# A fused matmul and rotary embedding: a new order in the head, and two more block pairs

## The chip, the core and the metric

The kernel runs on one core of a Trainium2 chip. The metric is the device time of one execution in microseconds (us), lower is better. Times before: 151.65 us median of three runs, 151.28 to 151.76. The engines are named as in the profile: PE (TensorE, matrix products; PEld are its weight loads), DVE (VectorE), ACT (ScalarE), POOL (GpSimd) and SP (SyncE, which here only issues DMAs).

## The reference

`x` is 16 x 512 x 768, `weight` 768 x 768, `cos` and `sin` 512 x 64, all float32; there are 12 heads of 64 columns.

```
y = np.matmul(x, weight).reshape(16, 512, 12, 64)
y1, y2 = y[..., :32], y[..., 32:]
out1 = y1 * cos1 - y2 * sin1      # cos1, sin1: the first 32 columns
out2 = y2 * cos2 + y1 * sin2      # cos2, sin2: the last 32
out  = np.concatenate([out1, out2], axis=-1).reshape(16, 512, 768)
```

Cosine and sine depend on the position in the sequence only, not on the batch or the head.

## The kernel before

**Tiles and groups.** The 8192 rows are cut into 64 tiles of 128 rows; a tile holds every fourth position of one batch, so that one set of cosine and sine rows serves it (`where`, L188). Four tiles, one from each of four batches, make a group; there are 16 groups. A group's result is 3072 columns wide and fills six banks of PSUM (`py`, L173). A tile needs six products of 128 rows of depth (`CHUNKS`, L133) for its 768 columns.

**The way of one tile.** SP loads it as float32 into one of ten buffers (`load`, L201). ACT casts it to float16 (`cast`, L236). PE transposes it in six 128 x 128 blocks (`turn`, L244) or, in the steady part, in twelve 64 x 64 blocks on two halves of the array's rows (`turn_rows`, L256). ACT copies it from PSUM (L185). PE multiplies it with the weights. DVE reads the banks and multiplies by cosine and by sine (`rope`, L412); POOL adds the two (L429), which gives the output in one of five buffers `ov`; ACT, at the end SP, stores it (`store`, L443).

**Block pairs.** Where `BLOCKS` (L137) names the second half of a group, its two tiles go another way. They are loaded in four quarters, permuted by the DMA, by SP in float32 (`xb`, then a cast on ACT, `cast_pair`, L274) or by POOL with the cast in the DMA (`xh`). DVE then transposes 32 x 32 blocks in one instruction (`turn_pair`, L282), into `xp`. PE does no transposes for them. Before, groups 5 to 14 have such a half, odd groups by SP, even ones by POOL.

**The order of products.** From tile 4 to tile 57 PE works in a row form (`walk`, `one`, `both`, L342 to L388): each product of depth 128 is split into two of depth 64, which run side by side on the two halves of the array's rows. The first half of the rows goes through three banks in the order 0, 1, 2, the second in the order 2, 0, 1 and 1024 columns later (`LAG`, L339). When both have finished a bank, `rope` is written for it: a unit of 512 columns and one of 1024 in each half of a group. Group 0 (`mm0`, L519) and the end run on the full array (`mm_piece`, L330).

**What sets the order around it.** Everything is written out by hand, in one list per engine; each engine works in order, and `Flow` (L17) places semaphores where data or buffers need them. In the loop over tiles (L639) `turns` writes transposes ahead by `T_AHEAD` = 3, `casts` by `C_AHEAD` = 5, `bturns` the block transposes of DVE by `B_AHEAD` = 4, `pool_loads` by `P_AHEAD` = 20, and `stores` (L607) holds the tile at which each store is issued. Loads of SP are written as buffers become free (`pump`, L491), in the order of `fetch` (L475).

**The head.** SP loads tiles 0 and 1, then weights and tiles in the order of L463, then cosine and sine, then the rest. Twelve products of zeros (`warm`) run first. Weight pieces are cast by DVE as they land, and group 0's products follow piece by piece. DVE makes the table of cosine and signed sine (`csn`, L557 to L561) ahead of the first `rope`.

**Buffers of the products.** `rope` writes its two products to `tq`, or to the space of the raw weights; from group 1 on there are three such buffers for halves of groups (`HOMES`, L171), so the products of one half wait for the additions of the half three before.

Of the kernel before, what the change touches and what calls it, by code (L numbers as in the profile page):

```python
# [12 lines left out]
MULT = mybir.AluOpType.mult  # L13
# [92 lines left out]
def kernel(  # L106
# [28 lines left out]


    BLOCKS = {}  # L137
    for g in range(5, 15):
        BLOCKS[g, 1] = "pool" if g % 2 == 0 and g >= 4 else "sp"

    def sbuf(name, shape, dt):
# [29 lines left out]
    HOMES0, HOMES, HOMESL = (0, 1024, 3072, 4096), (6144, 0, 3072), (0, 1024, 2048, 3072, 4096, 5120)  # L171
# [129 lines left out]
    def units(g):  # L301
        if g < LAST:
            cut = [2560] if g == LAST - 1 else []
            at = [0, 512, 1536, 2048] + cut + [3072]
            return [(c, z, py[:, c:z], [f"ps{b}" for b in range(c // 512, z // 512)],
                     "dve" if (g, c) == (LAST - 1, 2560) else "pool")
                    for c, z in zip(at, at[1:])]
        u = [(c, c + 512, py[:, c : c + 512], [f"ps{c // 512}"], "pool")
             for c in range(0, 2048, 512)]
        if g == LAST:  # L310
            for k, (home, bank) in enumerate([
                (py[:, 2048:2304], "ps4"), (py[:, 2560:2816], "ps5"),
                (pt_b[0][:, 0:256], "pt0"), (pt_b[1][:, 0:256], "pt1"),
            ]):
# [79 lines left out]
    def rope(g, u):  # L394
# [4 lines left out]
        if adder == "dve" and g == LAST:  # L399
            k = len(late)  # L400
            tq, keys = xs_b[k][:, 0 : 2 * w].rearrange("p (j n) -> p j n", j=2), [f"xs{k}"]
        elif 0 < g < LAST:
            lo = c0 % 1536
            if lo == 0:
                tq_of[0] = HOMES[ring("tq", len(HOMES))]
            tq, keys = products(tq_of[0], 1536, lo, lo + w)
            if tq_of[0] >= 6144:
                keys = keys + W_HOME
        else:
            homes = HOMESL if g else HOMES0  # L410
            tq, keys = products(homes[ring(f"tq{g}", len(homes))], w, 0, w)
        do("dve", lambda eng: eng.tensor_tensor(  # L412
            out=tq.rearrange("p j (h d) -> p j h d", d=D),
            in0=ps.rearrange("p (h d) -> p h d", d=D)
            .unsqueeze(1).broadcast_to((P, 2, nh, D)),
            in1=csn[:, :, r, :].unsqueeze(2).broadcast_to((P, 2, nh, D)),
            op=MULT), reads=banks + ["csn"], writes=keys)
        if g not in ov_of:
            ov_of[g] = ring("ov", NOV)
        o = ov_of[g]  # L420
# [39 lines left out]
        out=ident, in_=ident, compare_op=mybir.AluOpType.not_equal, fill=1.0,  # L460
        base=0, pattern=[[-1, P]], channel_multiplier=1), writes=["ident"])

    order = [0, 1, "w0", 2, "w1", "w2", 3, "w3", "w4", "w5"]  # L463
    for k in order:
        if isinstance(k, int):
            load(k)
        else:
            load_w(CHUNKS[int(k[1])])
    do("sp", lambda eng: eng.dma_start(
        out=csn[:, 0], in_=cos.rearrange("(p r) d -> p r d", r=SB)), writes=["cos"], dma="cos")  # L470
    do("sp", lambda eng: eng.dma_start(
        out=sin_sb, in_=sin.rearrange("(p r) d -> p r d", r=SB)), writes=["tq23"], dma="sin")
# [14 lines left out]
    fetched = [0]  # L487
    xs_used, xb_used = [0], [0]
    xs_sent, xb_sent = [4], [0]

    def pump():  # L491

# [12 lines left out]
                load_quarter(*j)  # L505
            fetched[0] += 1

    WARM = 12
    warmed = [0]

    def warm(k):
# [15 lines left out]
    def castx(i, e):  # L527
        cast(i, e)
        xs_used[0] += 1
# [3 lines left out]
    castx(0, "act")  # L533
    turn(0, "dve")
    castx(1, "act")
    warm(3)
    turn(1, "dve")
    castx(2, "act")
    cast_w(CHUNKS[0], "dve")
    for i in (0, 1):  # L540
        mm0(i, CHUNKS[0])
    turn(2, "act")
    castx(3, "act")
    for c in CHUNKS[1:3]:
        cast_w(c, "dve")
        for i in (0, 1):
            mm0(i, c)
    for c in CHUNKS[:2]:
        mm0(2, c)
    turn(3, "act")  # L550
    mm0(2, CHUNKS[2])
    for c in CHUNKS[3:5]:
        cast_w(c, "dve")
        for i in (0, 1, 2):
# [3 lines left out]
        out=csn[:, 1, :, 0:HD], in_=sin_sb[:, :, HD:D]), reads=["tq23"], writes=["csn1"])  # L558
    do("dve", lambda eng: eng.tensor_scalar_mul(
        out=csn[:, 1, :, HD:D], in0=sin_sb[:, :, 0:HD], scalar1=-1.0),  # L560
        reads=["tq23", "csn1", "cos"], writes=["csn"])  # L561
    assert not quarters
    pump()

    rows_on = [False]
    state = {"cast": 4, "turn": 4, "bturn": 0, "pool": 0}
    pairs = sorted(BLOCKS)
    pool_pairs = [p for p in pairs if BLOCKS[p] == "pool"]

# [50 lines left out]
    ROWS = QB * LAST - 2  # L620

    for i in (0, 1):
        mm0(i, CHUNKS[5])
    rope(0, U0[0])
    rope(0, U0[1])
    mm0(2, CHUNKS[5])
    rope(0, U0[2])
    casts(6)
    for c in CHUNKS[:3]:
        mm0(3, c)  # L630
    turns(5)
    for c in CHUNKS[3:5]:
        mm0(3, c)
    turns(6)
    mm0(3, CHUNKS[5])
    rope(0, U0[3])
    casts(8)

    for i in range(QB, NTILE):  # L639
        g, s = divmod(i, QB)  # L640
        us = units(g)
        done_to = (s + 1) * H
        rows_on[0] = QB <= i <= QB * LAST
        if i < ROWS:
            if s % 2 == 0:
                for r in range(2):
                    lines[r].extend(walk(i // 2, r))
            for n in range(1, 4):
                both((i - QB) * 4608 + n * 1536)
                if n == (1 if i > QB else 2):  # L650
                    turns(i + T_AHEAD, 1)
        if i == ROWS:
            both(NTILE * 4608)
        for n, p in enumerate(pieces(g, s)) if i >= ROWS else ():
            a, z, _, bank = p
            if n == 1 and i < QB * LAST:
# [62 lines left out]
```

## Time and profile before

| | |
|---|---|
| profiled execution | 151.73 us |
| its span, first to last instruction | 149.9 us |
| granted TensorE clock | 0.986 |
| PE, PEld busy | 140.8, 111.5 us (94%, 74%) |
| DVE, ACT, POOL busy | 126.4, 78.2, 122.8 us (84%, 52%, 82%) |
| DMA | 51.28 MB, mean 342 GB/s |

Shares are averages over a head, a steady part and a tail. What a stage is bounded by is read from what ends the waits there: the chain of waits gives that in order of time, and the timelines give each engine's work with the idle time before it and who ended it. Lines of a timeline are start, duration, engine, line, operation, tiles, shape and count; several instructions of one kind that follow each other are merged.

### The profile page before, as it was taken

The numbers are of one execution on the slowest core, as the hardware profiler recorded it, in microseconds if no ns is written. First come the engines' busy times: TensorE is split into PE (matmuls) and PEld (weight loads), VectorE is DVE, ScalarE is ACT, GpSimd is POOL, SyncE is SP. The second block draws the span as 40 slices with busy tenths as digits, with TensorE's granted clock in tenths as the row PEclk, the third lists the DMA queues.
The fourth block names the chain that finished last, engine by engine and source line by source line (L and its number), as shares of the span: only waits on it lengthen the run. The fifth ranks groups of instructions, "written<-read, shape, count | busy, mean of one in ns | idle before, by whom it ended". The sixth has DMA issues, their size and how long they took to land.

```text
span 149.9 us, 4381 instructions
## 1 busy us (share of the span) xinstructions
PE 140.8 (94%) x1926; PEld 111.5 (74%) x1926; DVE 126.4 (84%) x92; ACT 78.2 (52%) x92; POOL 122.8 (82%) x68
## 2 busy tenths in 40 slices
PE   6879999999999999999999999999999999999930
PEld 2435578888888888888888888888888888756620
DVE  0245998887888899999989998999989998999980
ACT  3453898778777924466262916093445626264000
POOL 1000396999989989999999999999996979999990
PEclk9999999999999999999999999999999999999995
DMA  4999999999999999999999999999999989996683
GB/s 129 343 398 402 405 398 397 319 380 341 333 358 389 357 354 325 380 397 279 330 361 407 262 346 352 363 321 333 365 364 387 388 338 390 393 387 240 247 314 105
DMA packets 27875, 51.28 MB, mean 342 GB/s; under 512 B 7504, under 2 KB 13392, under 8 KB 27856
## 3 DMA queue, kind: packets, MB, share of 16 engines
q1 hardware_dynamic: 14592, 27.92, 53.8%
q10 hardware_dynamic: 7824, 21.11, 36.0%
q0 software_dynamic: 5440, 1.97, 10.6%
q8 instruction: 15, 0.25, 0.7%
q14 instruction: 4, 0.03, 0.1%
HBM read 27.79 MB, written 25.17 MB: 353 GB/s over the span
## 4 chain that ended last, share of the span: by engine, by line
PE 79%; DVE 6%; DMA 4%; POOL 3%; issue 2%; SPq 1%; POOLq 0%
PE py L360 70%; DMA w_raw<-in_weight_dram 4%; PE py L335 4%; PE pt L266 4%; POOL ov L429 3%; DVE w_raw L412 2%; DVE tq L412 2%; SPq L205 1%; PE pt L251 1%; DVE ov L429 1%; SPq L227 1%; POOLq L675 0%; DVE w_sb L185 0%; SPq L714 0%; SPq L116 0%
## 5 line engine op out<-in xcount | busy, mean ns | idle before, releaser
L429 POOL TENSOR_TENSOR ov<-tq 128x1536 f32<-128x1536 f32 (+3 forms) x31 | 77.4, 2516 | 19.4 <-DVE tq L412 19.3
L360 PE MATMUL py<-w_sb,xt 64*128 64x512 f16 (+1 forms) x864 | 81.3, 323 | 0.0
L412 DVE TENSOR_TENSOR tq<-py,csn 128x1024 f32<-128x1024 f32 (+2 forms) x46 | 74.6, 1655 | 5.3 <-PE py L360 4.9
L360 PEld LDWEIGHTS py<-w_sb,xt 64*128 64x128 f16 x864 | 60.3, 94 | 10.7 <-DVE tq L412 0.4
L185 ACT COPY xt<-pt 128x768 f16<-128x768 f16 x42 | 33.5, 799 | 50.1 <-PE pt L266 48.8
L185 ACT CAST xc<-xs 128x768 f16<-128x768 f32 x44 | 38.9, 904 | 9.4 <-DMA xs<-in_x_dram 7.1
L360 PE MATMUL py<-w_sb,xp 64*128 64x512 f16 (+1 forms) x432 | 42.6, 323 | 0.0
L412 DVE TENSOR_TENSOR w_raw<-py,csn 128x1024 f32<-128x1024 f32 (+1 forms) x21 | 35.2, 1676 | 3.7 <-PE py L360 3.5
L429 POOL TENSOR_TENSOR ov<-w_raw 128x1536 f32<-128x1536 f32 (+1 forms) x11 | 33.8, 3073 | 3.2 <-DVE w_raw L412 3.2
L360 PEld LDWEIGHTS py<-w_sb,xp 64*128 64x128 f16 x432 | 30.7, 94 | 5.1
L335 PE MATMUL py<-w_sb,xt 128*128 128x256 f16 (+1 forms) x90 | 15.7, 323 | 1.4 <-DVE w_sb L185 1.1
L266 PEld LDWEIGHTS pt<-ident,xc 64*128 64x128 f16 x456 | 14.8, 95 | 1.7 <-ACT xc L185 0.6
L266 PE MATMUL pt<-ident,xc 64*128 64x64 f16 x456 | 14.8, 190 | 0.0
L335 PEld LDWEIGHTS py<-w_sb,xt 128*128 128x128 f16 x90 | 8.1, 98 | 7.1 <-DVE w_sb L185 2.7
L220 POOL DMA_DIRECT2D xh<-in_x_dram x20 | 11.7, 592 | 0.0
L185 ACT CAST xd<-xb 128x1536 f16<-128x1536 f32 x5 | 8.2, 1634 | 0.0
L185 DVE CAST w_sb<-w_raw 128x768 f16<-128x768 f32 x6 | 3.4, 558 | 3.6 <-DMA w_raw<-in_weight_dram 3.6
L294 DVE STREAM_TRANSPOSE xp<-xh 128x768 f32<-128x768 f32 x5 | 6.2, 1243 | 0.0
L514 PE MATMUL py<-tq 128*128 128x512 f16 x12 | 4.9, 570 | 1.4 <-DVE tq L457 1.4
L185 DVE COPY xt<-pt 128x768 f16<-128x768 f16 x2 | 1.1, 557 | 5.2 <-PE pt L251 5.2
L294 DVE STREAM_TRANSPOSE xp<-xd 128x768 f32<-128x768 f32 x5 | 4.8, 968 | 0.0
L335 PE MATMUL py<-w_sb,xp 128*128 128x512 f16 (+1 forms) x24 | 4.2, 327 | 0.0
(20 smaller groups left out, 18.1 us busy)
## 6 DMA issues: line engine op xcount, KB each, us to landing
xs<-in_x_dram SPq DMA_DIRECT2D x44, 384.0 KB, 16.5
out_dram<-ov ACTq DMA_DIRECT2D x41, 384.0 KB, 7.4
out_dram<-ov ACTq DMA_DIRECT2D x6, 768.0 KB, 6.3
xb<-in_x_dram SPq DMA_DIRECT2D x20, 192.0 KB, 16.1
out_dram<-ov SPq DMA_DIRECT2D x4, 768.0 KB, 5.1
w_raw<-in_weight_dram SPq DMA_DIRECT2D x6, 384.0 KB, 7.2
xh<-in_x_dram POOLq DMA_DIRECT2D x20, 96.0 KB, 12.3
out_dram<-ov SPq DMA_DIRECT2D x1, 384.0 KB, 2.9
```

Of the source, the lines that this page charges most:

```text
L185: eng.copy(out=o, in_=i_) if e == "act" else eng.tensor_copy(out=o, in_=i_)
L205: do(e, lambda eng: eng.dma_start(out=xs_b[k], in_=x[b].rearrange("(p r) h -> r p h", r=SB)[r]), writes=[f"xs{k}"], dma=f"xs{k}")
L220: do(e, lambda eng: eng.dma_start(out=dst[ts(q, R)], in_=src[r, q]), writes=[f"{name}q{q}"], dma=name)
L227: do(e, lambda eng: eng.dma_start(out=w_raw[:, t, h], in_=wv[t, h]), writes=[f"wr{t}{h}"], dma=f"w{t}{h}")
L251: do("pe", lambda eng: eng.transpose(pt[:, t, h, :], src[:, t, h, :], ident), reads=[f"xc{c}", "ident"], writes=[f"pt{k}"], tick=(t, h) == ...
L266: do("pe", lambda eng: eng.transpose(pts[r][:, t, h, :], src[rows, t, h, :], ident[rows, rows]), reads=[f"xc{c}", "ident"], writes=[f"pt{r ...
L294: do("dve", lambda eng: eng.transpose(out=dst, in_=src), reads=rd, writes=[f"xp{z}"])
L335: do("pe", lambda eng: eng.matmul(ps, get(t, h), w_sb[:, t, h, a - s * H : z - s * H], start=start, stop=stop), reads=[key, f"w{t}{h}"], w ...
L360: do("pe", lambda eng: eng.matmul(py[:, a:z], get(t, h)[rows], w_sb[rows, t, h, a - s * H : z - s * H], start=start, stop=not opens and en ...
L412: do("dve", lambda eng: eng.tensor_tensor(out=tq.rearrange("p j (h d) -> p j h d", d=D), in0=ps.rearrange("p (h d) -> p h d", d=D) .unsque ...
L429: do(adder, lambda eng: eng.tensor_tensor(out=ov_b[o][:, ds(c0, w)].rearrange("p (h t d) -> p h t d", t=2, d=HD), in0=tq[:, 0].rearrange(" ...
L514: do("pe", lambda eng: eng.matmul(py[:, ts(b, 512)], cold[:, 0:P], cold, start=True, stop=warmed[0] < WARM - 6), reads=["tq0"], writes=[f" ...
```

## The change

- **Loads.** Tile 4 is loaded behind the last weight piece, ahead of sine and cosine, and sine goes ahead of cosine. The table's two parts have keys of their own, so that the first `rope` waits for both parts and for cosine.
- **Head.** One warm product less; the first weight cast goes ahead of the copy of tile 1; tile 2 gets its third weight piece with tiles 0 and 1. Tile 5 is cast by POOL. Tile 4 is transposed in the middle of tile 3's products.
- **Group 0** has six `rope` units of 512 columns instead of 512, 1024, 512 and 1024, with bank 5 ahead of bank 4.
- **Group 1** begins on the full array: tiles 4 and 5 (`FIRST` is 6) are written by `mm_piece`, and the transposes of tiles 5, 6 and 7, in the form of `turn_rows`, stand between their products. The row form begins with tile 6.
- **Block pairs** begin with group 3: the second halves of groups 3 (by SP) and 4 (by POOL) are added. Up to tile 18 (`EVEN`) the block transposes are written one tile later, and transposes and casts are placed by even and odd tiles.
- **Stores.** Up to group 9, store number k is issued at tile 12 + k; before, at tile 5 + 47 k / 40, rounded down.

```diff
-    for g in range(5, 15):
+    for g in range(3, 15):
         BLOCKS[g, 1] = "pool" if g % 2 == 0 and g >= 4 else "sp"
...
             at = [0, 512, 1536, 2048] + cut + [3072]
+            if g == 0:
+                at = [*range(0, 3073, 512)]
...
-            homes = HOMESL if g else HOMES0
-            tq, keys = products(homes[ring(f"tq{g}", len(homes))], w, 0, w)
+            tq, keys = products(HOMESL[ring(f"tq{g}", len(HOMESL))], w, 0, w)
...
-            op=MULT), reads=banks + ["csn"], writes=keys)
+            op=MULT), reads=banks + ["cos", "csn1", "csn2"], writes=keys)
...
-    order = [0, 1, "w0", 2, "w1", "w2", 3, "w3", "w4", "w5"]
+    order = [0, 1, "w0", 2, "w1", "w2", 3, "w3", "w4", "w5", 4]
...
     do("sp", lambda eng: eng.dma_start(
+        out=sin_sb, in_=sin.rearrange("(p r) d -> p r d", r=SB)), writes=["tq23"], dma="sin")
+    do("sp", lambda eng: eng.dma_start(
         out=csn[:, 0], in_=cos.rearrange("(p r) d -> p r d", r=SB)), writes=["cos"], dma="cos")
-    do("sp", lambda eng: eng.dma_start(
-        out=sin_sb, in_=sin.rearrange("(p r) d -> p r d", r=SB)), writes=["tq23"], dma="sin")
...
-    WARM = 12
+    WARM = 11
...
     castx(1, "act")
-    warm(3)
+    cast_w(CHUNKS[0], "dve")
     turn(1, "dve")
+    warm(2)
     castx(2, "act")
-    cast_w(CHUNKS[0], "dve")
...
     pump()
+    castx(4, "act")
+    castx(5, "pool")
...
-                i, n = 5 + (47 * (QB * g + s)) // 40, 1
+                i, n = 3 * QB + QB * g + s, 1
...
-    rope(0, U0[0])
-    rope(0, U0[1])
+    for k in (0, 1, 2):
+        rope(0, U0[k])
     mm0(2, CHUNKS[5])
-    rope(0, U0[2])
-    casts(6)
+    rope(0, U0[3])
     for c in CHUNKS[:3]:
         mm0(3, c)
     turns(5)
-    for c in CHUNKS[3:5]:
+    casts(7)
+    for c in CHUNKS[3:]:
         mm0(3, c)
-    turns(6)
-    mm0(3, CHUNKS[5])
-    rope(0, U0[3])
-    casts(8)
+    for k in (5, 4):
+        rope(0, U0[k])
...
-        if i < ROWS:
+        full = i < FIRST or i >= ROWS
+        if not full:
...
-                if n == (1 if i > QB else 2):
+                if n == 1 and (i % 2 or i >= EVEN):
                     turns(i + T_AHEAD, 1)
...
-        for n, p in enumerate(pieces(g, s)) if i >= ROWS else ():
+        for n, p in enumerate(pieces(g, s)) if full else ():
...
             for c in CHUNKS:
+                if i < FIRST and (n, c) == (s, CHUNKS[3]):
+                    turns(i + 2 + s, 1)
...
-        bturns(i + B_AHEAD)
-        turns(i + 1 + (T_AHEAD if i > QB else 2), 1)
+        bturns(i + (B_AHEAD if i >= EVEN else 3))
+        if i == QB:
+            casts(8)
+        if i >= EVEN or i % 2 == 0:
+            turns(i + (4 if i >= EVEN else 3), 1)
...
-        casts(i + 1 + (C_AHEAD if i > QB else 4), 1 + i % 2)
+        if i >= EVEN:
+            casts(i + 1 + C_AHEAD, 1 + i % 2)
+        elif i % 2:
+            casts(i + C_AHEAD, 2)
```

More of the change, by code (lines that the diff above doesn't have):

```diff
@@ L169, in products @@
         return v[:, :, lo:hi], sorted(keys)
-    HOMES0, HOMES, HOMESL = (0, 1024, 3072, 4096), (6144, 0, 3072), (0, 1024, 2048, 3072, 4096, 5120)
+    HOMES, HOMESL = (6144, 0, 3072), (0, 1024, 2048, 3072, 4096, 5120)
     ov_b = [sbuf(f"ov{i}", [P, QB * H], FP32) for i in range(NOV)]
@@ L486 @@
             fetch.append(quarters.pop(0))
-    fetched = [0]
+    fetched = [1]
     xs_used, xb_used = [0], [0]
-    xs_sent, xb_sent = [4], [0]
+    xs_sent, xb_sent = [5], [0]
     def pump():
@@ L543 @@
     castx(3, "act")
[L544 to L547, printed above, removed]
+    cast_w(CHUNKS[1], "dve")
+    for i in (0, 1):
+        mm0(i, CHUNKS[1])
     for c in CHUNKS[:2]:
         mm0(2, c)
+    cast_w(CHUNKS[2], "dve")
+    for i in (0, 1, 2):
+        mm0(i, CHUNKS[2])
     turn(3, "act")
-    mm0(2, CHUNKS[2])
     for c in CHUNKS[3:5]:
@@ L560 @@
         out=csn[:, 1, :, HD:D], in0=sin_sb[:, :, 0:HD], scalar1=-1.0),
-        reads=["tq23", "csn1", "cos"], writes=["csn"])
+        reads=["tq23"], writes=["csn2"])
     assert not quarters
     pump()
+    castx(4, "act")
+    castx(5, "pool")
     rows_on = [False]
-    state = {"cast": 4, "turn": 4, "bturn": 0, "pool": 0}
+    state = {"cast": 6, "turn": 4, "bturn": 0, "pool": 0}
     pairs = sorted(BLOCKS)
@@ L619 @@
     C_AHEAD, T_AHEAD, B_AHEAD, P_AHEAD = 5, 3, 4, 20
-    ROWS = QB * LAST - 2
+    FIRST, EVEN, ROWS = QB + 2, 4 * QB + 2, QB * LAST - 2
+    at[:] = [2 * 4608, 2 * 4608 + LAG]
     for i in (0, 1):
         mm0(i, CHUNKS[5])
-    rope(0, U0[0])
-    rope(0, U0[1])
+    for k in (0, 1, 2):
+        rope(0, U0[k])
     mm0(2, CHUNKS[5])
-    rope(0, U0[2])
-    casts(6)
+    rope(0, U0[3])
     for c in CHUNKS[:3]:
@@ L653 @@
             both(NTILE * 4608)
-        for n, p in enumerate(pieces(g, s)) if i >= ROWS else ():
+        for n, p in enumerate(pieces(g, s)) if full else ():
             a, z, _, bank = p
-            if n == 1 and i < QB * LAST:
+            if n == 1 and ROWS <= i < QB * LAST:
                 turns(i + T_AHEAD, 1)
             for c in CHUNKS:
+                if i < FIRST and (n, c) == (s, CHUNKS[3]):
+                    turns(i + 2 + s, 1)
                 mm_piece(i, p, c, c == CHUNKS[0], c == CHUNKS[-1],
```

## The prediction

> **What bounds the kernel now.** I read the page's busy slices first, then the chain that ended last in order of time, then the timelines of TensorE, VectorE and GpSimd, last the DMA landings.
>
> From the page, busy tenths in 40 slices:
> ```profile
> PE   6879999999999999999999999999999999999930
> DVE  0245998887888899999989998999989998999980
> POOL 1000396999989989999999999999996979999990
> DMA  4999999999999999999999999999999989996683
> ```
> Four resources look full, so shares do not tell which one ends the others' waits. The chain does (start, us, what):
> ```profile
> 10.04 0.57 DVE w_sb L185
> 10.61 0.05 issue
> 10.65 1.47 PE py L335 x8
> ...
> 29.37 0.20 PE pt L266 x11
> 29.57 1.96 PE py L360 x18
> ...
> 37.87 0.20 PE pt L266 x11
> ...
> 56.68 0.17 PE pt L266 x10
> ...
> 64.83 0.17 PE pt L266 x10
> ...
> 129.85 2.28 DVE tq L412 x2
> ```
> From 10.65 to 129.85 us the chain is TensorE without a gap; before it stand the weight loads, after it VectorE and GpSimd. A stage is worth what it takes off TensorE's row. Two periods are seen: a group of four tiles all transposed on TensorE goes from 29.37 to 37.87, 8.50 us, and a group whose second half is a block pair from 56.68 to 64.83, 8.15 us. So a transposed tile costs 0.175 and its products 1.95 us.
>
> TensorE's timeline, head and tail (start, us, engine, line):
> ```profile
> 17.60 0.50 PE L251 MATMUL pt<-ident,xc 128*128 128x128 f16 x6
> 18.37 1.73 PE L360 MATMUL py<-w_sb,xt 64*128 64x512 f16 x10
> 22.83 0.37 PE L266 MATMUL pt<-ident,xc 64*128 64x64 f16 x11
> ...
> 130.60 2.12 PE L335 MATMUL py<-w_sb,xp 128*128 128x512 f16 x12
> 132.65 0.35 PE L266 MATMUL pt<-ident,xc 64*128 64x64 f16 x12
> 132.94 2.12 PE L335 MATMUL py<-w_sb,xp 128*128 128x256 f16 x12
> ```
> VectorE's:
> ```profile
> 15.28 6.75 DVE L412 TENSOR_TENSOR tq<-py,csn 128x1024 f32<-128x1024 f32 x4
> 27.95 2.29 DVE L412 TENSOR_TENSOR tq<-py,csn 128x2048 f32<-128x2048 f32 x1 [0.26 <-PE py L360]
> 53.18 0.97 DVE L294 STREAM_TRANSPOSE xp<-xd 128x768 f32<-128x768 f32 x1
> ```
>
> **Part by part.** The profiled execution took 151.73 us, 1.83 around its span of 149.9; it is 0.08 above the median of 151.65. All marks below are in its time.
>
> *Block pairs.* Four tiles (14, 15, 18, 19) lose their transposes on TensorE: two periods go from 8.50 to 8.15, **-0.70**. ScalarE loses four casts of 0.90 and four copies of 0.80 and gains a pair cast of 1.63; it is busy 52%, so that is worth nothing. VectorE gains two block transposes, 0.97 and 1.24: in these groups it idled 0.19 to 0.54 us four times a period, some 1.5 us, against 0.35 of period lost and one transpose, which fits; where they stand is costed below.
>
> *Head.* Up to the last weight piece nothing can gain: w5's cast ends at 14.51 and TensorE's first matmul on it starts at 14.58 in both, since the six weight loads keep their place; one warm matmul less and w0's cast ahead of the second transposed copy lie before the wait for w1 (landed 9.05). Then, with 0.216 us from start to start for a 512 and 0.109 for a 256: last piece for tiles 0 to 2, 0.98; half of tile 3, 0.98; transposes of tile 4, 0.34; rest of tile 3, 0.98: 17.84, about 17.9 with ScalarE's copy of tile 4 (0.54 from the transposes' start, then 0.80). Before, group 1 began at 18.37 with tile 5 turned as well. Now tiles 4 and 5 run on the full array, 2 x 1.95, and tiles 5, 6 and 7 are turned between their pieces in the row form. That form's price among full matmuls is in the tail: twelve products from 130.60 would end at 132.55, the next starts at 132.94, so 0.38 a tile, not 0.175. 17.9 + 3.90 + 3 x 0.38 + 0.11 for the step to the row form gives 23.05. Before, the row form reaches tile 6 at 23.05 too (22.83 and tile 8's transposes), with tile 8 turned already. So the earlier start is spent: **+0.17**. By the price in the row stretch it would be -0.44, and the sum 0.6 lower; I take the tail's, whose neighbours are the same. The Trainium skill (TensorEngine Tiling (Array Packing), Key Properties) says that changing the tiling mode drains TensorE, which speaks against these three insertions; by that rule the tail's price holds and the sum stands at 151.55, without it at 150.95. The tail rows side with it.
>
> *What covers the head.* With tile 4 (0.98 a tile) ahead, sine lands near 15.3 and cosine near 15.6 instead of 14.65 and 14.29; the products of group 0 start at 15.9, not 15.28. Six of 512 columns follow each other at 1.14, so banks come free at 17.1, 18.2, 19.4, 20.5, 21.7 (bank 5) and 22.8 (bank 4); they are wanted at 17.9, 19.6, 21.3, 23.05, 23.5 and 24.3. Cost 0; past 0.8 us of further delay it is one for one. Tile 5's cast goes to GpSimd, behind a landing at 16.6 and wanted at 18.55: 1.95 us of room. The trace has no such cast there. Bounds: 0.56 (VectorE's cast of this size), and 1.85, by the line through GpSimd's additions of 512 (1.33) and 1024 (2.37), with 13% for the strided read (ScalarE's 0.90 against 0.80) 2.1. I take 1.4, nearer the additions, as it is the same engine: cost 0, at the upper end 0.15.
>
> *GpSimd afterwards.* Cast to 18.0, six additions of 1.27 to 25.7, four issues for pair (4,1) 2.4 to 28.1, first addition of group 1 to 31.6, issues for (6,1) to 34.0, second addition to 37.45. Behind it waits VectorE's first product of group 3, which reuses that buffer, near 39.1: 1.6 of room. Later periods take 4 x 3.44 + 2.3 = 16.06 of 16.3, and the idle 0.74, 0.32, 0.24, 0.24, 1.52 and 1.00 that it shows from 56 to 122 us takes up the lag before the tail. Cost 0.
>
> *Where the two transposes stand.* They are queued behind the 1024-column product of the half before, not ahead of it as at 53.18. That product starts 4.90 after its half with two turns in it (27.95 - 23.05); the next instruction 2.17 after it; 0.1 on to TensorE. Pair (3,1): the half of tiles 10 and 11 starts at 23.05 + 4 x 1.95 + 4 x 0.175 = 31.55; product 36.45, transpose 38.62 to 39.6, usable 39.7; TensorE gets to tile 14 at 31.55 + 7.80 + 0.35 = 39.70. Pair (4,1): half 39.8, product 44.7, transpose 46.87 to 48.1, usable 48.2; TensorE is there at 47.95. Waits 0.1 and 0.25: **+0.35**. 0.2 either way in each mark gives 0 to 0.8.
>
> *Loads and stores.* ScalarE's first store goes from 23.29 to about 37, six stores later by then; SP's four quarters of (3,1) come behind tile 8 and delay tiles 9 to 13 by up to 2 us, against 3.2 to 4.8 between landing and cast. Stores then go one a tile, not 0.85, and level with before near tile 50. One more pair by GpSimd costs its queue's 4.04 us a read MB (10.6% of 149.9 for 3.93) against SP's 2.89 (53.8% for 27.92): 0.9 us, and the SP pair at most as much. Loads of tiles 49 and 53 land 2.9 and 3.2 ahead of their casts: 1 left. Buffers of stored groups are wanted five tiles after their stores. Cost 0.
>
> *Tail.* Same order; VectorE waits for TensorE at 125.39 (0.41), so the shift goes through.
>
> Sum: -0.70 + 0.17 + 0.35 = -0.18: 151.55 of the profiled kind, 151.47 against the median. **Forecast 151.5**, within 0.3% (0.46 us, about what a measurement of this kernel tells from no change).
>
> **Rivals.** *The pairs are in time.* If VectorE's products start 0.3 earlier against TensorE than my marks, only -0.70 + 0.17 is left: 151.2 profiled, 151.1 against the median, down to 150.9 with cheaper insertions. For it: waits this small hang on marks of 0.2. Against: two pairs would have to fit at once.
>
> *Slower: GpSimd's cast.* Tile 5's transposes stand in TensorE's queue ahead of half of tile 4, so each us of the cast beyond 1.95 is one on the path; beyond 2.6 it is slower by 0.3%. At 3.0: 152.6. For it: no row of such a cast. Against: the additions' line ends at 2.1. The Trainium skill (GPSIMD Engine Reference, Engine selection and the cycle accounting before it) calls one-input work roughly line rate; an estimate from its 1.03 to 1.8 cycles an element is 0.7 to 1.2 us, by which this rival falls and the sum stays; no run here shows it yet.
>
> *Slower: late quarters.* (4,1) is issued from 25.7 to 28.1 and wanted at 46.9; landings took 7.7 to 18.6 us, so the last comes by 46.1 at worst. At 21 us VectorE, and TensorE behind it, lose 1.6: 153.1. Without stores until 37 us it should be sooner. Loads short near tile 50 are of this kind too.
>
> *The head gains nothing by itself* is my own forecast.
>
> **How the numbers follow.** Forecast 0.42; pairs in time 0.27; cast 0.11; late quarters or loads 0.13; rest 0.07, evenly. Faster 0.28, same 0.42, slower 0.30. The range, 150.9 to 152.8, goes from the first rival's end past the cast's. The forecast's own is 151.2 to 152.0.
>
> **What would show it.** Group 1 begins near 17.9; 0.38 around each of three row-form turns there; row form from about 23.05; periods of 8.15 in groups 3 and 4 plus a wait for VectorE's transposes at tiles 14 and 18; the tail shifted whole. Wrong if GpSimd's cast is over 2 us, TensorE waits for sine or cosine, or a wait shows near tile 50.

## The result and the profile after

The changed kernel takes **153.44 us** (median of four runs, 153.06 to 153.99), the kernel before beside it 151.70 (151.28 to 151.93, four runs). The ratio is 1.012, 95% interval [1.009, 1.015]: slower by 1.74 us, where 151.5 was forecast, and above the upper end of the range, 152.8. The profiled execution took 153.99 us with a span of 152.2 at a granted clock of 0.995; it stands 0.55 above the median, so terms of its trace are compared with the trace of before, not with the medians. Here and in the experiments a run more than 1.5% above the fastest of its kernel is left out of the ratio, so a ratio need not be the quotient of two medians.

The page of the changed kernel, busy time of each engine and busy tenths in 40 slices, with the rate of the DMAs:
```profile
PE 142.2 (93%) x1859; PEld 99.6 (65%) x1859; DVE 128.1 (84%) x96; ACT 73.7 (48%) x84; POOL 126.3 (83%) x75
...
DMA  4999999999999999999999999999999999999883
GB/s 127 313 388 406 394 202 232 242 285 247 238 339 307 388 307 326 360 400 337 342 350 385 355 350 353 370 385 332 355 360 410 410 413 409 417 410 369 331 320 103
```
TensorE is busy 1.4 us longer than before (140.8), though four tiles' transposes are gone. The DMA row reads 9 all along, yet between the sixth and the eleventh slice, about 19 to 42 us, it moves 202 to 285 GB/s.

The chain that ended last shows the place. First the head (start, us, what):
```profile
19.41 0.28 PE pt L266 x12
19.70 1.41 PE py L337 x9
21.10 0.28 PE pt L266 x12
...
22.80 0.28 PE pt L266 x12
...
23.83 1.94 PE py L362 x16
```
The three row-form turns among full products are there, one every 1.69 us (1.41 + 0.28), and the row form starts at 23.83 (23.77 in TensorE's timeline), where 23.05 was forecast. Then the same view from there on:
```profile
26.13 0.81 ACT xt L185
...
26.99 0.35 PE pt L266 x12
27.34 3.24 PE py L362 x30
30.58 0.22 PE pt L266 x12
...
30.82 0.81 ACT xt L185
...
31.68 0.35 PE pt L266 x12
...
35.52 0.81 ACT xt L185
...
44.17 0.81 ACT xt L185
```
Before, this stretch was TensorE without a gap. Now ScalarE's copy of transposed tiles stands in it four times, each time between one group of twelve transposes and the next. Two tiles take 4.69 (26.13 to 30.82) and 4.70 us (30.82 to 35.52); before, half of the period of 8.50, 4.25. So each of the four costs some 0.445 us (the fourth stands among block pairs and is taken to cost the same).

The waits of TensorE and of its weight loads name the same releaser (engine, line, waited for: us in total, times, longest us):
```profile
PE pt L266 <- ACT xt L185: 1.1, 4, 0.3
```
```profile
PEld pt L266 <- ACT xt L185: 2.6, 5, 0.5
PEld py L362 <- DVE xp L294: 0.5, 2, 0.3
```
The third line is the two waits for VectorE's block transposes, at tiles 14 and 18. The chain shows the second, and behind it the period that was forecast:
```profile
49.44 1.15 DVE xp L294
...
50.64 0.83 PE py L362 x6
...
53.11 5.85 PE py L362 x56
...
61.26 5.85 PE py L362 x56
...
132.13 2.25 DVE tq L413 x2
```
From 53.11 to 61.26 is 8.15 us, and nothing but TensorE stands in the chain until the tail begins with VectorE's product at 132.13. Before, that product began at 129.85.

**The account of these 2.28 us.** The row form starts 0.78 later than forecast. From there to the tail it is 108.30 us, against the 106.80 that before took from the same point of the work (23.05 to 129.85): +1.50. Its parts: tile 8's turn, still to do here and done there, 0.175; two periods shorter by 0.35, -0.70; four copy waits, 4 x 0.445 = 1.78; and what is left, 0.25 (0.31 with the timeline's 23.77), which is put down to the block transposes. Of these, -0.70 and the waits for block transposes are in the forecast's sum, and tile 8's turn is in its head; the copy waits and the later start are not.

**Where the copy waits come from.** `turn_rows` writes its twelve transposes into both banks of `pt` at once (L261), and the copy reads both (L269). So a turn can't start until the copy of the turn before it has ended. Before, the turns stood one per tile, 2.1 us apart. The changed loop writes them, up to tile 18, at the end of each even tile and after the first third of the next odd one. TensorE's timeline has such a pair (start, duration, idle time before):
```profile
30.42 0.35 PE L266 MATMUL pt<-ident,xc 64*128 64x64 f16 x12
30.59 0.82 PE L362 MATMUL py<-w_sb,xt 64*128 64x256 f16 x9
31.68 0.35 PE L266 MATMUL pt<-ident,xc 64*128 64x64 f16 x12 [0.26 <-ACT xt L185]
```
From the start of the first turn it is 0.40 us to the start of the copy (30.82), then 0.81 of copy and 0.05 of signalling: the second turn starts 1.26 after the first. TensorE has work for 0.825 of them, the turn itself (0.175) and a third of a tile (0.65 of products). The difference, 0.435, is the 0.445 but for 0.01.

### The profile page after: what moved, and what is told of

It reads as the page before. It is cut to its first block, busy times and chain, and to the rows that moved or that the text cites. A ratio compares the mean times of both kernels' runs of the same rounds, so it can differ in the third digit from the quotient of the medians.

```text
span 152.2 us, 4257 instructions
## 1 busy us (share of the span) xinstructions
PE 142.2 (93%) x1859; PEld 99.6 (65%) x1859; DVE 128.1 (84%) x96; ACT 73.7 (48%) x84; POOL 126.3 (83%) x75
## 4 chain that ended last, share of the span: by engine, by line
PE 75%; DVE 9%; DMA 4%; POOL 3%; issue 2%; ACT 2%; SPq 1%; POOLq 0%; DVEq 0%
PE py L362 62%; PE py L337 8%; DVE tq L413 5%; DMA w_raw<-in_weight_dram 4%; PE pt L266 4%; POOL ov L430 3%; DVE w_raw L413 2%; ACT xt L185 2%; SPq L205 1%; DVE xp L294 1%; DVE ov L430 1%; POOLq L686 0%; PE pt L251 0%; DVE w_sb L185 0%; SPq L227 0%
## 5 line engine op out<-in xcount | busy, mean ns | idle before, releaser
L362 PE MATMUL py<-w_sb,xt 64*128 64x256 f16 (+1 forms) x720 | 68.6, 323 | 0.0
L185 ACT COPY xt<-pt 128x768 f16<-128x768 f16 x38 | 30.4, 800 | 52.6 <-PE pt L266 49.8
L362 PEld LDWEIGHTS py<-w_sb,xt 64*128 64x128 f16 x720 | 46.4, 94 | 14.3 <-issue 0.4
L362 PE MATMUL py<-w_sb,xp 64*128 64x256 f16 (+1 forms) x528 | 51.6, 323 | 0.1
L185 ACT CAST xc<-xs 128x768 f16<-128x768 f32 x39 | 34.2, 903 | 13.6 <-DMA xs<-in_x_dram 9.5
L362 PEld LDWEIGHTS py<-w_sb,xp 64*128 64x128 f16 x528 | 33.4, 94 | 10.9 <-DVE xp L294 0.5
L430 POOL TENSOR_TENSOR ov<-w_raw 128x1536 f32<-128x1536 f32 (+1 forms) x11 | 33.7, 3072 | 2.0 <-DVE w_raw L413 2.0
L337 PE MATMUL py<-w_sb,xt 128*128 128x256 f16 (+1 forms) x114 | 20.3, 324 | 0.6 <-DVE w_sb L185 0.5
L266 PEld LDWEIGHTS pt<-ident,xc 64*128 64x128 f16 x420 | 12.3, 95 | 4.8 <-ACT xt L185 2.6
L220 POOL DMA_DIRECT2D xh<-in_x_dram x24 | 14.0, 591 | 0.0
L266 PE MATMUL pt<-ident,xc 64*128 64x64 f16 x420 | 12.1, 191 | 1.1 <-ACT xt L185 1.1
```

The costliest lines, as they stand in the source:

```text
L185: eng.copy(out=o, in_=i_) if e == "act" else eng.tensor_copy(out=o, in_=i_)
L220: do(e, lambda eng: eng.dma_start(out=dst[ts(q, R)], in_=src[r, q]), writes=[f"{name}q{q}"], dma=name)
L266: do("pe", lambda eng: eng.transpose(pts[r][:, t, h, :], src[rows, t, h, :], ident[rows, rows]), reads=[f"xc{c}", "ident"], writes=[f"pt{r ...
L337: do("pe", lambda eng: eng.matmul(ps, get(t, h), w_sb[:, t, h, a - s * H : z - s * H], start=start, stop=stop), reads=[key, f"w{t}{h}"], w ...
L362: do("pe", lambda eng: eng.matmul(py[:, a:z], get(t, h)[rows], w_sb[rows, t, h, a - s * H : z - s * H], start=start, stop=not opens and en ...
L430: do(adder, lambda eng: eng.tensor_tensor(out=ov_b[o][:, ds(c0, w)].rearrange("p (h t d) -> p h t d", t=2, d=HD), in0=tq[:, 0].rearrange(" ...
```

## The experiments

Each kernel is compared with the one before on its own chip; the kernel before took 151.97 us beside the kernels marked e, 151.55 beside f, 151.73 beside g and 151.83 beside h.

| kernel | us | ratio, 95% interval | tail begins, us |
|---|---|---|---|
| after | 153.44 | 1.012 [1.009, 1.015] | 132.13 |
| after, second turn later (e1) | 154.18 | 1.0161 [1.0122, 1.0199] | 132.45 |
| after, stores of before (e2) | 154.49 | 1.0181 [1.0131, 1.023] | 134.39 |
| before, pairs from group 3 (e3) | 154.30 | 1.0165 [1.0122, 1.0208] | 132.53 |
| before, turns in pairs (e4) | 153.88 | 1.0143 [1.0113, 1.0174] | 132.07 |
| after, even placement from tile 6 (f1) | 151.48 | 1.0003 [0.9978, 1.0027] | 130.27 |
| new head alone (f3) | 152.19 | 1.0034 [1.0014, 1.0054] | 131.15 |
| before, late stores (f4) | 151.65 | 1.0012 [0.9992, 1.0032] | 129.81 |
| before, pairs and late stores (f5) | 153.50 | 1.0112 [1.0075, 1.0148] | 130.87 |
| as f5, late quarters (g1) | 151.84 | 0.9989 [0.9960, 1.0018] | 128.89 |
| before, new load order (g2) | 152.16 | 1.0030 [1.0013, 1.0047] | 130.29 |
| new head, old load order (g3) | 152.87 | 1.0070 [1.0044, 1.0096] | 131.07 |
| as f1, late quarters (g4) | 151.90 | 1.0007 [0.9985, 1.0029] | not read |
| before, new opening (h1) | 151.99 | 1.0003 [0.9989, 1.0016] | 129.63 |
| as f1, old opening (h2) | 152.05 | 1.0021 [0.9998, 1.0045] | 129.52 |
| as f1, old opening, late quarters, cast 8 early (h3) | 151.76 | 1.0013 [0.9989, 1.0037] | 129.58 |

"Tail begins" is the start of VectorE's first product of the tail in the profiled execution; 129.85 in that of before shown above. The profiled execution of e2 took 156.25 us, 1.8 above its median; its rows are read for the place of a wait only. That of g4 ran at a granted clock of 0.564; one landing is read from it and nothing else.

### Do the paired turns cost it?

**In the kernel before, the turns of tiles 10 to 19 put in pairs, and nothing else (e4).**
```diff
-                if n == (1 if i > QB else 2):
+                if n == (1 if i > QB else 2) and (i % 2 or not 6 <= i < 18):
                     turns(i + T_AHEAD, 1)
...
-        turns(i + 1 + (T_AHEAD if i > QB else 2), 1)
+        if not 6 <= i < 18:
+            turns(i + 1 + (T_AHEAD if i > QB else 2), 1)
+        elif i % 2 == 0:
+            turns(i + T_AHEAD, 1)
```


> The kernel before with the transposes of tiles 10 to 19 written in pairs a third of a tile apart, as the change writes them, and nothing else. Theory one: five copy waits of about 0.45 us, so 153.7 to 154.0, 2.0 to 2.3 above before. Theory two: the pairing costs nothing, 151.7.

Measured: 1.0143, which is 2.17 us for five pairs, 0.43 each. The chain, which before had TensorE alone there:
```profile
34.06 0.81 ACT xt L185
...
34.91 0.35 PE pt L266 x12
35.26 3.24 PE py L360 x30
38.50 0.22 PE pt L266 x12
...
38.75 0.81 ACT xt L185
```
It has the same rows, 0.81, 0.35, 3.24, 0.22, and the same 4.69 from copy to copy. The cost needs nothing else of the change.

**In the changed kernel, the second turn of each pair put at the end of its tile (e1).**
```diff
-                if n == 1 and (i % 2 or i >= EVEN):
+                if n == 1 and i >= EVEN:
...
-        if i >= EVEN or i % 2 == 0:
-            turns(i + (4 if i >= EVEN else 3), 1)
+        turns(i + (4 if i >= EVEN else 3), 1)
```


> The changed kernel with one tile's transposes at the end of every tile, from tile 6 to tile 17, instead of two tiles' transposes a third of a tile apart at every other tile; nothing else is changed. Theory one (the second of two turns waits for ScalarE's copy out of the two transpose banks, 4 times some 0.45 us): the waits of TensorE for the copy go, and the time falls by 1.5 to 1.8 us, to 151.6 to 152.0. Theory two (the time is lost to loads that come late, since the quarter loads and the missing stores lower what the DMA moves between 18 and 42 us): no change, 153.4.

Measured: 1.0161, no gain. TensorE's copy wait changed its place instead: products wait for it now, and no longer turns (TensorE's waits):
```profile
PE py L362 <- ACT xt L185: 1.7, 4, 0.4
```
and the chain runs through the copy as before, now ahead of products:
```profile
27.80 0.81 ACT xt L185
...
28.74 1.51 PE py L362 x13
```
The row form's second half of rows begins a pair of tiles with bank 2, which belongs to the pair's second tile (`walk`, order 2, 0, 1). That tile is therefore wanted 1024 columns after the first, and a turn at the end of the tile ahead comes too late for it. The experiment did not free the path, it delayed the second turn; it says that turns can't be spread by moving that one later.

**In the changed kernel, the even placement begun at tile 6 instead of 18 (f1):** turns, casts and block transposes stand as in the steady part.
```diff
-    FIRST, EVEN, ROWS = QB + 2, 4 * QB + 2, QB * LAST - 2
+    FIRST, EVEN, ROWS = QB + 2, QB + 2, QB * LAST - 2
```


> The changed kernel with its steady placement of transposes, casts and block transposes beginning at tile 6 instead of tile 18 (EVEN is 6): every tile is turned three tiles ahead, one a tile, as in the kernel before. Theory one (copy waits of the paired turns): they go, 1.5 to 2 us less than the changed kernel, 151.5 to 152. Theory two (the loads are what comes last; the pairing is only fitted to their late landing): tiles 10 to 13 land at 25.5 to 33 us, later than this order asks for them, TensorE waits for casts instead of copies, and the time stays within 0.7 us of the changed kernel's 153.4.

Measured: 1.0003 [0.9978, 1.0027], 1.96 us less than the changed kernel by the medians (1.8 by their ratios to before). The chain of that kernel:
```profile
26.24 0.21 PE pt L266 x12
26.45 1.95 PE py L362 x21
28.40 0.17 PE pt L266 x12
```
From here to the tail neither the copies nor the block transposes are left in it, and a turn takes 0.17 to 0.21 again, one in each 2.1 to 2.2 us. Ahead of it stand one copy (22.95) and the cast of tile 8 (23.75), for which TensorE idles 0.21. One placement decides nearly the whole loss. That it is the turns, and not the casts that f1 moves with them, is what e4 shows.

### The loads: pairs without the rest

**Before, with pairs from group 3 (e3); the changed kernel with the stores of before (e2); before with the late stores alone (f4); pairs and late stores (f5).** The edits are these two, one or both, in either direction:
```diff
-    for g in range(5, 15):
+    for g in range(3, 15):
...
-                i, n = 5 + (47 * (QB * g + s)) // 40, 1
+                i, n = 3 * QB + QB * g + s, 1
```


> The kernel before with block pairs from group 3 on and nothing else. By the prediction's term for the block pairs alone (two periods of 8.15 instead of 8.50, transposes of VectorE written early as in the later groups, so no wait for them): 151.0, 0.7 below before. Rival: the quarter loads cost the DMA more than is hidden (stores start at tile 5 here), loads come late and TensorE waits: 151.7 or more.

> The changed kernel with the stores at the tiles of before (from tile 5 on, 0.85 a tile). Theory one (copy waits): the time stays at 153.2 to 153.7, with the four copy waits in the chain as they were. Theory two (loads late for want of DMA throughput after the deferred stores): the loads of tiles 24 to 57 land 2 us or more ahead of their casts again, and the time falls by 1 us or more.

> The kernel before with the first store at tile 12 and one a tile from there. The prediction's step: no cost, 151.7. If the DMA loses throughput while no store runs beside the loads (220 to 266 GB/s between 18 and 42 us in the changed kernel against 337 to 403 before), the loads lose the lead again later and the time rises, by up to 1 us.

> The kernel before with block pairs from group 3 on and the late stores, with its own head and placement. With the stores out of the way tiles 10 to 13 should land at 25.5 to 31.5 us, as in the changed kernel, instead of 26 to 35 us. Theory two (the pairs alone lost 2.5 us to late loads): most of that goes, 151.0 to 152.0. If the quarter loads by themselves hold the loads up whatever the stores do: 153.5 or more.

Measured: pairs alone lose, 1.0165. In the waits of e3 and its chain the loads have taken TensorE's place:
```profile
ACT xc L185 <- DMA xs<-in_x_dram: 34.3, 19, 3.5
```
```profile
17.17 18.01 DMA xs<-in_x_dram
...
35.20 0.35 ACT xc L185
```
A row tile (13), issued at 17.17, lands 18 us later, and ScalarE's cast waits for it; behind it the periods are 8.15 again. The late stores cost nothing by themselves (f4, 1.0012, an interval with 1 in it). With the pairs they may help: f5 is at 1.0112 where e3 is at 1.0165, but the two intervals overlap. The stores of before in the changed kernel (e2) make it no better, 154.49 where either expectation had less, and in its profiled execution the chain is in the loads until 63 us. So the late stores came at no cost, as the forecast took them; that the pairs need them is not shown.

In f5 the loads are not on the path. Its chain is TensorE, with one stop:
```profile
26.29 1.26 issue
27.55 1.28 PE py L360 x11
```
"Issue" means that the profile shows nothing that TensorE waited for. What follows are products of tiles 6 and 7; the transposes of tile 10 come a microsecond later, and tile 10's cast had ended at 26.17. The trace of e3 has the same stop, ahead of the same product, beside its waits for the loads:
```profile
PE py L360 <- issue: 1.8, 1, 1.8
```
One thing that moves with it is the first 16-KB packet of the instruction queue (q8 on the page): it starts at 24.61 in f5 and 25.00 in e3, at 22.40 to 22.62 in before, f4 and g1, which have no such stop. Instructions that come late behind the quarters would fit. No run shows it, and in the changed kernel, e1, e2 and f1, whose products stand in another order, the packet is late too (23.72 to 24.83) and there is no such stop.

**As f5, with the quarters of (3,1) queued behind tiles 12 and 13 instead of 8 to 11 (g1).**
```diff
-        if soon and i >= max(2, soon[0][0] - 1) * QB:
+        if soon and i >= max(3, soon[0][0] - 1) * QB:
```


> The kernel before, with block pairs from group 3, single stores from tile 12 on, and the quarters of (3,1) queued behind the loads of tiles 12 and 13 instead of those of tiles 8 to 11. Theory: the 768-B quarter pieces among the loads of tiles 8 to 11 are what made tiles 10 and 11 land too late in the run with pairs and late stores (1.0112); with them behind, tiles 10 and 11 land with 0.5 us or more to spare, the wait of 1.3 us at tile 10 is gone, and what is left is the gain of two periods, -0.70: 150.8 to 151.3 us, ratio 0.995 to 0.998. Rival: the loads are late whatever stands among them, and it stays at 1.011 (153.2). Second rival: the quarters now land too late for their own cast, and tile 14 waits: 152 to 153, with the wait at the block transpose of (3,1) instead of at tile 10.

Measured: 0.9989 [0.996, 1.0018]; f5 was 1.0112. The stop of 1.26 us is gone, and tiles 10 and 11 land at 21.2 and 22.2, 3.3 and 3.8 us ahead of their casts, where in f5 they landed at 25.3 and 28.0 with 0.02 to spare. So the quarters among the row tiles are what made them late. But the stop was not at tile 10, as the expectation had it, so how much of the 1.2% comes from the loads stays open. The time misses the expectation too, 0.995 to 0.998. The stretches show what they do (us, then busy time and instruction count of PE, PEld, DVE, ACT and POOL, the granted clock, the DMA share and GB/s). First before:
```profile
18.00:23.00 5.00, 5.00 (x82) 3.44 (x81) 4.81 (x4) 4.77 (x7) 4.22 (x3) 1.00 1.04 403
23.00:28.00 5.00, 5.00 (x95) 4.26 (x90) 4.01 (x4) 4.38 (x6) 3.59 (x2) 1.00 1.03 341
```
the changed kernel:
```profile
18.00:23.00 5.00, 5.00 (x61) 2.62 (x58) 5.00 (x5) 3.67 (x5) 5.00 (x5) 1.00 1.09 242
23.00:28.00 5.00, 4.73 (x71) 3.27 (x67) 3.76 (x4) 3.79 (x5) 5.00 (x7) 1.00 1.06 220
```
and g1:
```profile
18.00:23.00 5.00, 5.00 (x85) 3.64 (x86) 4.81 (x4) 4.49 (x6) 4.49 (x3) 1.00 1.05 386
23.00:28.00 5.00, 5.00 (x84) 4.26 (x82) 4.01 (x4) 4.64 (x7) 4.98 (x6) 1.00 1.08 237
```
Where the quarters run and no store yet, the rate falls to some 220 to 240 GB/s at nearly the same share; g1 puts that stretch behind the tiles that were short. The missing stores have a part in the rate: from 28 to 36 us, with the same order of loads, before moves 369 GB/s with stores among them and f4 245 without, and f4 is not slower.

**As f1, with the same later quarters (g4).**

> The changed kernel with steady placement from tile 6 (1.0003), and the quarters of (3,1) queued behind the loads of tiles 12 and 13. Theory: in that run loads were just in time (tile 12 with 0.02 us to spare); with the quarters later tiles 9 to 13 land 1 to 2 us earlier, but the chain there went by PE, so the time stays: 151.3 to 151.5, ratio 0.998 to 1.000. Rival: loads still cost about 0.3 to 0.5 there (waits too short to see), and the time falls to 151.0 to 151.2, ratio 0.996 to 0.998. Second rival: (3,1) lands too late and the time rises above 151.8.

Measured: 1.0007 [0.9985, 1.0029], no different from f1. In f1 the loads were just in time already.

### The head

**The new head with the pairs and stores of before, placed as in f1 (f3); the same with the load order of before (g3); before with only the new load order (g2).** The order is this edit:
```diff
-    order = [0, 1, "w0", 2, "w1", "w2", 3, "w3", "w4", "w5"]
+    order = [0, 1, "w0", 2, "w1", "w2", 3, "w3", "w4", "w5", 4]
...
+    do("sp", lambda eng: eng.dma_start(out=sin_sb, ...
     do("sp", lambda eng: eng.dma_start(out=csn[:, 0], ...
-    do("sp", lambda eng: eng.dma_start(out=sin_sb, ...
```


> The new head alone: the loads' order, the six products of group 0 and group 1 begun on the full array, with block pairs from group 5 on, the stores and the steady placement of before. By the prediction's step for the head, 0.2 above before: 151.9. If the turns in row form between full products cost more, or the later weights seen in the changed kernel (0.2 to 0.6 us) belong to this head: 152.2 to 152.6.

> The head of the changed kernel with the stores and blocks of before, its steady placement from tile 6, and the load order of before (cosine, sine, then tile 4). Beside it stands the same kernel with the new order, 1.0034. Theory: most of the head's +0.5 us is the later landing of the weights that goes with the order; with the old one w5 lands at 13.9 and the time is 151.5 to 151.7 (ratio 1.000 to 1.001), unless the cast of tile 4 now waits for its load. Rival: the head costs 0.5 by its row-form turns among full products (three at 0.39 against 0.175) and its later row form, whatever the order: 152.0 to 152.2, ratio 1.003 to 1.004.

> The kernel before with the load order of the changed kernel alone: tile 4 right behind the last piece of weight, sine ahead of cosine. Theory: the later weights (w5 landed at 14.06 to 14.53 in every kernel with the new order, at 13.80 to 14.02 with the old) come from this order; w5 lands at about 14.4 here, and the time rises by 0.3 to 0.5: 151.9 to 152.1, ratio 1.002 to 1.003. Rival: they come from the rest of the head (other casts and a smaller warm-up), w5 lands at 13.9 and the time stays at 151.5 to 151.7.

Measured: the head alone costs 1.0034 with the new order and 1.0070 with the old one. Some 0.25 us of both is the experiment's own: tile 8's turn now stands after the first third of tile 6, and waits for its cast, which ends at 24.7 (as in f1). The rest, 0.25 to 0.8, is the head's cost, against 0.17 forecast. The theory that the order delays the weights falls: with the order alone the last weight piece lands at 14.02, with the new head and the old order at 14.31. That g2 loses 0.45 us all the same has another reason, shown by its chain:
```profile
7.07 8.67 DMA csn<-in_cos_dram
...
15.77 0.24 DVE csn L559
...
16.03 3.43 DVE tq L412 x2
```
In the kernel before, with units of 512 and 1024 columns in group 0, cosine behind tile 4 puts VectorE's first products on the path. The changed head has six units of 512 there and no such wait: the forecast's cover held.

**The opening (first weight cast ahead of the second copy, one warm-up product less): alone in before (h1), and taken back in f1 (h2).**
```diff
-    WARM = 12
+    WARM = 11
...
-    warm(3)
+    cast_w(CHUNKS[0], "dve")
     turn(1, "dve")
+    warm(2)
     castx(2, "act")
-    cast_w(CHUNKS[0], "dve")
```


> The kernel before with the opening of the changed one alone: the first weight cast ahead of the copy of tile 1 on VectorE, and eleven warm-up products instead of twelve. In seven profiled executions with the old opening w5 landed at 13.68 to 14.02, in six with the new at 14.06 to 14.53, whichever load order they had. Theory: the opening itself makes the weights land later (the 3-KB packets between 6 and 10 us take longer beside VectorE's or TensorE's other order): w5 lands at 14.2 to 14.5 and the time rises by 0.3 to 0.6, to 151.9 to 152.2, ratio 1.002 to 1.004. Rival: it is something else of the changed kernel (the length of its program, the casts behind 14 us, chance): w5 lands at 13.7 to 14.0 and the time stays, ratio 0.999 to 1.001.

> The changed kernel with steady placement from tile 6 (1.0003, w5 at 14.33), and the opening of the kernel before. Theory that the opening delays the weights: w5 lands at 13.7 to 14.0, the first row-form product moves 0.4 earlier, and the time falls to 151.0 to 151.3, ratio 0.996 to 0.998. Rival: w5 stays at 14.2 to 14.5 and the time at 151.4 to 151.7, ratio 1.000.

Measured: h1 1.0003, with the last weight piece at 13.72. h2 1.0021 [0.9998, 1.0045], with that piece at 13.46, and the row of TensorE some 0.75 us earlier than in f1 all the way to the tail (129.52 against 130.27). So the opening alone doesn't delay the weights; in the one pair of traces where it is taken back they come 0.9 earlier, and the times of the runs don't follow. The two theories are each half refuted.

**All mends at once (h3):** f1, the old opening, the later quarters, and this:
```diff
         if i == QB:
-            casts(8)
+            casts(9)
```


> All mends at once: the changed kernel with steady placement from tile 6, the opening of before, the quarters of (3,1) behind the loads of tiles 12 and 13, and the cast of tile 8 ahead of the copy of tile 7. By the sum: before 151.6, +0.17 to 0.34 for group 1 begun by the full array (three turns at 0.39 against 0.175 and the unexplained 0.17), -0.70 for the two groups of pairs, and nothing else left: 151.1 to 151.3, ratio 0.996 to 0.998, with the first row-form product at 23.1 to 23.4, no wait of TensorE behind it before the tail, and tiles 10 to 13 landing with over 1 us to spare. Rival: the head of the changed kernel costs 0.5 to 1.0 for another reason (it did so alone, 1.0034 and 1.007): 151.4 to 151.9, ratio 0.999 to 1.002.

Measured: 1.0013 [0.9989, 1.0037], the rival's time. The row form starts at 23.11 as expected and tiles 10 to 13 land 2.2 to 5.1 us ahead of their casts, but the cast of tile 8, put ahead, made a wait of its own in the head's chain:
```profile
18.85 0.80 ACT xt L185
19.65 1.60 ACT xc L185 x2
21.25 0.71 ACT xt L185
...
22.01 0.35 PE pt L266 x12
```
Two casts in a row on ScalarE hold up the copy for which the next turn waits. No kernel here is shown to be faster than the one before; g1 comes nearest.

## Why the prediction was wrong

**The step that failed** is the one on the two transposes, where it sets the marks: "the half of tiles 10 and 11 starts at 23.05 + 4 x 1.95 + 4 x 0.175". It gave every turn in groups 1 to 4 the 0.175 of the steady rows, though the diff changes where they are written (`i % 2 or i >= EVEN`). The price of a turn was read from a stretch with one turn per tile, evenly placed, and used where two stand 0.65 us apart. The rows that would have given it were there: the copy's 0.80, the 0.54 from a turn's start to its copy, and 1.95 a tile, so 0.65 a third. The forecast used all three elsewhere. The step cost 4 x 0.445 = 1.78 us in the trace; e4 gives 0.43 a pair in the kernel before, and f1 takes it away. No rival named it.

**"The six weight loads keep their place"** was right of the order and wrong of the time: w5 landed at 14.53, not 13.92, and that is 0.6 of the 0.78 by which the row form starts late. Its cause stays open. It is there from the first piece on: w0, issued at 1.86 here and 1.85 before, landed at 7.50, not 6.47. With new head and new opening together the last piece landed at 14.06 to 14.53 in six traces (g3 among them, 14.31), with the old head or the old opening at 13.46 to 14.02 in ten; but the execution of g4 at the clock of 0.564 has both too, and there it landed at 13.88. Five of the six have the same head to the letter and lie 0.47 apart, with one execution of each, so chance is not ruled out. Neither the order (g2, g3) nor the opening (h1) does it alone, and the runs of h2 didn't become faster with it.

**The block pairs, -0.70:** right. The periods are 8.15 from 53 us on in the changed kernel and from 35 us on in f1, and in g1 the tail begins at 128.89, 0.96 ahead of before, 0.3 of it by an earlier third weight piece (9.70 against 10.01). In the times of g1's runs, though, only 0.17 us of it is seen, inside an interval of -0.6 to +0.3.

**The waits for VectorE's block transposes, +0.35:** right in kind and near in size; two waits, 0.5 us in the weight loads' row and 0.25 of what is left in the account. All its marks came 2.1 to 2.7 us later, on VectorE and TensorE alike.

**The head, +0.17:** the price of the turns was right: 0.39 each (1.69 from turn to turn less 1.30 of products) against 0.38. So changing between the array's two forms shows here as it did in the tail of before: 0.39 among full products, 0.175 among products of its own form. The rule of the Trainium skill that the forecast weighed (TensorEngine Tiling (Array Packing), Key Properties) says that a change of tiling mode drains TensorE; these rows agree with it, without showing the drain by itself. The start is 0.17 later than the marks and the weights explain. Some 0.06 of that lies between the two views, 23.83 in the chain and 23.77 in the timeline, where 23.05 is a mark of the timeline. The other 0.1 fits tile 4's copy: it ends at 18.46 and the first product of tile 4 starts at 18.61, 0.15 later, where the forecast allowed 0.02 between them and TensorE was ready at about 18.44.

**GpSimd's cast:** the upper bound of 2.1 us was far off. In the groups of the changed kernel:
```profile
L185 POOL CAST xc<-xs 128x768 f16<-128x768 f32 x1 | 0.9, 884 | 15.8 <-PE py L337 15.8
```
0.884 us, where 1.4 was taken. The rival built on it fell. The estimate of 0.7 to 1.2 us from the Trainium skill (GPSIMD Engine Reference, Engine selection and the cycle accounting before it) holds; the additions, which read two inputs, were the wrong neighbours.

**GpSimd's lag, sine and cosine, the quarters of (4,1):** hidden, as forecast. Its first addition of group 1 starts at 28.08 (28.1 forecast), and the last quarter of (4,1) landed by 41.6, where 46.9 was the limit.

**Loads and stores, "cost 0":** right for this kernel by luck, from marks that were wrong. Tiles 9 to 13 were to come up to 2 us later than before; they came 3.7 to 7.6 later, and landed with 0.02 to 1.2 us to spare where the forecast left 1 to 3. Tiles 49 and 53 had 0.02 instead of 1, tile 45 too. TensorE waited for none of them. That the copy waits had made it late by then is not the reason that is shown: f1 has none of these waits, tile 12 lands there with 0.02 to spare, and TensorE does not wait for loads either. In e3 the same loads were on the path.

So, of +1.74 us measured: four copy waits about +1.75, the waits for block transposes about +0.25, the head with its later weights +0.25 to +0.8, the pairs -0.70. The terms add to 1.55 to 2.1; the two in the middle are remainders, not measured alone.

## What to carry over

A price read from a row holds for the spacing in which the row stands: when a change moves instructions that share a buffer with no second copy (here both banks of PSUM), work out the distance between each two of them against the copy that frees the buffer, before any other term. A gain on TensorE of 0.35 us a group is worth having only if the loads of that stretch have more to spare than the other form of load takes from them; look at landing against use, tile by tile, and at what a wait near a late load names, which need not be the load (f5). And an experiment that moves one wait has to be read for the wait that it makes (e1, f3, h3).

## What the runs showed of the hardware

- The DMA share doesn't tell the rate. From 18 to 28 us it is 1.03 to 1.04 before and 1.06 to 1.09 after, while 403 and 341 GB/s became 242 and 220. From 18 to 23 us neither kernel stores yet. In that stretch and the next SP's queue holds 3072-byte row packets mixed with 768-byte pieces of the quarters: a row packet took 206 to 226 ns, against 124 when the rows run alone, and a piece 62.
- Most kernels with pairs from group 3 scatter more than those without, in the runs that count in the ratios: f4 ran at 151.19 to 152.50 us and h1 at 151.49 to 152.34, g1 at 150.40 to 152.61 and h2 at 151.37 to 153.06; but f3, without these pairs, at 151.56 to 153.03. Their loads have 0.02 us to spare at several tiles in the traces (49 and 53 in g1, seven from tile 29 on in h3), which would explain why a gain of 0.70 in the chain does not show in the median. That is argued, not shown.
